# RWKV's weighted key-value scan on one core: constant rows by GpSimd's queue, later converting loads, and earlier state steps

## The chip, the cores and the metric

The kernel runs on one core of one Trainium2 chip. The metric is the device time of one execution in microseconds (us), lower is better. A core has a matrix engine (TensorE, PE in the profile), a vector engine (VectorE, DVE), a scalar engine for activations (ScalarE, ACT), GpSimd (POOL) and a fifth engine, SyncE (SP), which here only issues transfers. They run side by side and each works through its own list in order. Transfers between the chip's main memory and the on-chip memory are started by an engine that issues them and are then carried out by the core's 16 DMA engines.

## What is computed

For each of 16 sequences, 2048 steps and 256 channels, a weighted running mean of v is kept, with weights exp(k) that decay by w with each step; the current step has the extra weight u. The reference keeps the running maximum pp so that no exponential overflows:

```python
# w, u: [256]; k, v, output: [16, 2048, 256], all float32
for t in range(seq_len):
    ww = u + k[t]
    qq = max(pp, ww)
    output[t] = (exp(pp - qq) * aa + exp(ww - qq) * v[t]) / (exp(pp - qq) * bb + exp(ww - qq) + 1e-8)
    ww = pp - w + k[t]
    qq = max(ww, k[t])
    aa = exp(ww - qq) * aa + exp(k[t] - qq) * v[t]
    bb = exp(ww - qq) * bb + exp(k[t] - qq)
    pp = qq
```

## The kernel before

Time is cut into 16 chunks of 128 steps; a chunk of four sequences is one *slot*, so there are 64 slots, four to a chunk. In a slot n

- k and v (512 KB each) are loaded; k is rounded by DVE (`round_k`) and v converted to bf16 by DVE (`cast_v`), except that for every fourth slot from 11 on the transfer itself converts v[...];
- PE forms the exponents from k and from the rows of w and u (`logs`), ACT exponentiates them (`exps`), DVE multiplies by v (`times_v`);
- PE sums over half chunks (`sums`); once per chunk a chain of small operations on ACT, DVE, GpSimd and PE carries the state on (`copy_sums`, `turn`, `state_logs`, `state_frames`, `state_scan`, `state_offsets`, `state_weights`, `state_chain`, `turn_back`) and GpSimd injects it into rows of the exponentials by four small transfers (`inject`);
- ten slots later (LAG) PE forms denominator and numerator (`den`, `num`), ACT the reciprocal as Ln and Exp (`recip`), DVE the product (`mult`), and SP stores the result.

The parts that the change touches (cuts marked):

```python
AHEAD, LAG, RING = 6, 10, 12
kpool = ...tile_pool(name="kpool", bufs=AHEAD)
vpool = ...tile_pool(name="vpool", bufs=5)
vbpool = ...tile_pool(name="vbpool", bufs=4)        # v as bf16

def v_mode(n):
    return "dma" if n >= LAG and n % 4 == 3 else "dve"

def load_k(n, queue=SP): ...                         # 512 KB
def load_v(n, queue=SP):
    if v_mode(n) == "dma":
        VB[n] = vbpool.tile([128, 4, Dm], BF16, tag="vb", name="vb")
        K(POOL.dma_start(out=VB[n], in_=rows_of(v, n)))      # converts
    else:
        vr_of[n] = vpool.tile([128, 4, Dm], F32, tag="vr", name="vr")
        K(queue.dma_start(out=vr_of[n], in_=rows_of(v, n)))

def load(n):
    load_k(n)
    load_v(n)
# ...
K(POOL.memset(wuf, 0.0))
fill(idle, 0.0); fill(M1, -1.0); fill(I1, 0.0)       # fill: DVE memset
load_k(0, SP)
load_row(SC, 0, 0, w)                                # 2 rows of wuf
load_row(SP, 1, 2, u)
for n in range(1, AHEAD):
    load_k(n); load_v(n - 1)
# ... GpSimd: iota for COf, selects for M1, I1, COf (two)
# ... DVE: NLE and NLZ from M1 and I1, fills of Sel and OH, CO from COf
# ... GpSimd: six selects for Sel
# ...
def state_start(): ...       # DVE fills for the first chunk's state
def out_matrices(*names): ...# DVE: L, Id, LN, IdN from Lx and I1
# ...
idle_matmuls(10, MISC)
round_k(0)
fill(Lx, 1.0)                # and three selects on GpSimd
K(SC.activation(WU, wuf..., ACT.Copy))
logs(0); round_k(1); cast_v(0)
for n in range(LAG):
    load_v(n + AHEAD - 1)
    load_k(n + AHEAD)
    exps(n)
    if n % 4 == 0 and n: sums(n - 1)
    small_work(n, "act"); small_work(n, "logs")
    logs(n + 1)
    if n % 4: sums(n - 1)
    small_work(n, "pe")
    idle_matmuls(2, NUMB)
    times_v(n)
    small_work(n, "chain")
    round_k(n + 2)
    small_work(n, "round")
    cast_v(n + 1)
    if n == 2: state_start(); out_matrices("Id")
    if n == 6: out_matrices("L", "IdN", "LN")
load_v(LAG + AHEAD - 1)
for n in range(LAG, NP):
    if n + AHEAD < NP: load(n + AHEAD)
    # ... num, den, exps, recip, mult, round_k(n + 2), cast_v(n + 1),
    # ... store, times_v(n), logs(n + 1), sums; small_work between
# ... eleven more slots of outputs alone
```

`small_work(n, place)` runs the state steps that a plan puts in this place of slot n. For the first two chunks (slots 0 to 7) frames, scan and offsets are DVE's; later GpSimd has frames and offsets.

Of the kernel before, what the change touches and what calls it, by code (L numbers as in the profile page):

```python
# [15 lines left out]
def kernel(  # L16
# [10 lines left out]
    PE, DVE, SC, POOL, SP = nc.tensor, nc.vector, nc.scalar, nc.gpsimd, nc.sync  # L27

    B, T, Dm = k.shape
    HS = 64  # L30
# [3 lines left out]
    NP = 4 * NST  # L34
    RING = 12
    AHEAD = 6
    LAG = 10
# [16 lines left out]
    def v_mode(n):  # L54
        return "dma" if n >= LAG and n % 4 == 3 else "dve"

    def rows_of(x, n):
        c, p = divmod(n, 4)
        return x[4 * p:4 * p + 4, c * TC:(c + 1) * TC, :].rearrange("n t d -> t n d")

    def load_k(n, queue=SP):
        kr_of[n] = kpool.tile([128, 4, Dm], F32, tag="kr", name="kr")
        K(queue.dma_start(out=kr_of[n], in_=rows_of(k, n)))
# [4 lines that stand above are left out]
            K(POOL.dma_start(out=VB[n], in_=rows_of(v, n)))  # L68
        else:
            vr_of[n] = vpool.tile([128, 4, Dm], F32, tag="vr", name="vr")  # L70
            K(queue.dma_start(out=vr_of[n], in_=rows_of(v, n)))

    def load(n):
        load_k(n)
        load_v(n)

    def matrix(name, dt):
        return consts.tile([128, 128], dt, tag=name, name=name)  # L80

    def fill(ap, value):
        K(DVE.memset(ap.bitcast(F32) if ap.dtype == F32R else ap, value))

    GE, NE = ALU.is_ge, ALU.not_equal

    def select(ap, cmp, fill, base, cm, pattern):
        K(POOL.affine_select(out=ap, in_=ap, pattern=pattern, compare_op=cmp,
                             fill=fill, base=base, channel_multiplier=cm))

    M1, I1, Lx, COf = [matrix(x, F32) for x in ("M1", "I1", "Lx", "COf")]
# [3 lines left out]
    OH = consts.tile([128, 56], BF16, tag="OH", name="OH")  # L95
    Sel = consts.tile([128, 3, 2, 2, 4, 2], F32, tag="Sel", name="Sel")
    def load_row(eng, r, g0, x):
        K(eng.dma_start(out=wuf.rearrange("(g r) n d -> r g n d", r=32)[r, g0:4], in_=bass.AP(
            tensor=x.tensor, offset=x.offset, ap=[[0, 4 - g0], [0, 2], list(x.ap[0])])))
# [2 lines left out]
    fill(idle, 0.0)  # L102
    fill(M1, -1.0)
    fill(I1, 0.0)
    load_k(0, SP)
    load_row(SC, 0, 0, w)
    load_row(SP, 1, 2, u)
    for n in range(1, AHEAD):
        load_k(n)
        load_v(n - 1)  # L110
# [6 lines left out]
    for g in (2, 3):  # L117
        select(COf, NE, 1.0, -32 * g - 1, 1, [[0, 128]])


    NLE, NLZ, CO = matrix("NLE", F32R), matrix("NLZ", F32R), matrix("CO", F32R)
    K(DVE.tensor_scalar(NLE, M1, 0.5, None, ALU.add))
    for h in range(2):
        fill(NLE[HS * h:HS * h + HS, HS * (1 - h):HS * (2 - h)], 0.0)
    K(DVE.tensor_tensor(NLZ, NLE, I1, ALU.add))
    fill(Sel, 0.0)
    fill(OH, 0.0)
    for h in range(2):
        fill(OH[HS * h:HS * h + HS, 24 + h:25 + h], 1.0)
        fill(OH[HS * h:HS * h + 1, 32 + h:33 + h], 1.0)  # L130
    K(DVE.tensor_copy(CO, COf))
    for j, r in ((0, 0), (1, 8), (2, 64)):
        for h in range(2):
# [4 lines left out]
    def out_matrices(*names):  # L138
        if "L" in names:
            for h in range(2):  # L140
                fill(Lx[HS * h:HS * h + HS, HS * (1 - h):HS * (2 - h)], 0.0)
        for name in names:
            x, f = I1 if name[0] == "I" else Lx, RS if name[-1] == "N" else 1.0
            mats[name] = matrix(name, BF16)
            K(DVE.tensor_single_scalar(mats[name], x, f, op=ALU.mult))
# [18 lines left out]
    def round_k(n):  # L164
        km = consts.tile([128, 4, Dm], F32R, tag=f"km{n % 2}", name="km") if n < 2 else KM[n - 2]
        K(DVE.tensor_copy(km, kr_of.pop(n)))  # L166
        KM[n] = km
# [20 lines left out]
    def exps(n):  # L188
        if n < TURNS:
            for q in range(2):  # L190
                K(SC.activation(ez(n)[:, q], half(n, q), ACT.Exp))  # L191
        else:
            K(SC.activation(ez(n)[:, 0:2], PS[:, 0:4, :].rearrange("p (q i) x -> p q i x", q=2), ACT.Exp))  # L193
# [26 lines left out]
    def state_start():  # L220
        fill(CB_of[0], 0.0)
        K(DVE.memset(LL_of[0][:, 0, :, 0:1], -100.0))
        K(DVE.memset(LL_of[1][:, 1, :, 2:3], 0.0))
        for F in F_of:
            K(DVE.memset(F[:, :, 0:1], -1.0e30))
        K(DVE.memset(AB_of[0][:, :, 0, :], 0.0))
# [124 lines left out]
    def mult(n, bank, i):  # L351
        rd = RD[n]
        K(DVE.tensor_mul(rd[:, i, :], bank, rd[:, i, :]))  # L353
# [13 lines left out]
    for c in range(NST):  # L367
        s = 4 * c + 3
        plan = [(s + 1, "act" if s + 1 < LAG else "recip", copy_sums), (s + 1, "pe", turn),
                (s + 2, "act", state_logs), (s + 2, "mid", state_frames), (s + 2, "scan", state_scan), (s + 2, "scan", state_offsets),  # L370
                (s + 3, "recip", state_weights), (s + 3, "chain", state_chain),
                (s + 4, "nums", turn_back), (s + 4, "mid", inject), (s + 4, "mid", state_next)]
        if c == 0:
            plan = [(s + 1, "act", copy_sums), (s + 1, "pe", turn), (s + 2, "act", state_logs),
                    (s + 2, "round", state_frames), (s + 2, "round", state_scan), (s + 2, "round", state_offsets),
                    (s + 3, "act", state_weights), (s + 3, "round", state_chain),
                    (s + 4, "logs", turn_back), (s + 4, "logs", inject), (s + 4, "round", state_next)]
        if c == 1:
            plan = [(s + 1, "act", copy_sums), (s + 1, "pe", turn), (s + 2, "act", state_logs),
                    (s + 2, "round", state_frames), (s + 2, "round", state_scan), (s + 2, "round", state_offsets)] + plan[6:]  # L380
        if c == NST - 1:
            plan = [(s + 1, "copy", copy_sums), (s + 1, "turn", turn),
                    (s + 1, "post", state_logs), (s + 1, "mid", state_frames), (s + 1, "mid", state_scan), (s + 1, "mid", state_offsets),
                    (s + 2, "post", state_weights), (s + 2, "first", state_chain),
                    (s + 3, "turn", turn_back), (s + 3, "first", inject)]
        for slot, where, f in plan:
            later.setdefault((slot, where), []).append((f, c))

    def small_work(n, where):
        for f, c in later.pop((n, where), []):  # L390
            f(c)
# [4 lines left out]

    idle_matmuls(10, MISC)
    round_k(0)
    fill(Lx, 1.0)
    select(Lx, GE, 0.0, -1, -1, [[1, 128]])  # L400

    for h in range(2):
        select(Lx, NE, 1.0, -(HS * h + HS - 1), 1, [[0, 128]])
    K(SC.activation(WU, wuf.rearrange("p n d -> p (n d)"), ACT.Copy))
    logs(0)
    round_k(1)
    cast_v(0)
    for n in range(LAG):

        load_v(n + AHEAD - 1)  # L410
        load_k(n + AHEAD)
        exps(n)
        if n % 4 == 0 and n:
            sums(n - 1)
        small_work(n, "act")
        small_work(n, "logs")
        logs(n + 1)
        if n % 4:
            sums(n - 1)
# [4 lines that stand above are left out]
        round_k(n + 2)  # L424
        small_work(n, "round")
        cast_v(n + 1)
        if n == 2:
            state_start()
            out_matrices("Id")
        if n == 6:  # L430
            out_matrices("L", "IdN", "LN")
    load_v(LAG + AHEAD - 1)
    for n in range(LAG, NP):

        q, qp = n - LAG, n - LAG - 1
        if n + AHEAD < NP:
            load(n + AHEAD)
        if qp >= 0:
            num(qp, NUMB, 0)
        den(q)  # L440
        small_work(n, "nums")

        if n % 2 == 0:
            sums(n - 1)
        exps(n)
        small_work(n, "act")
        recip(q, lambda: small_work(n, "recip"))
        if qp >= 0:
            mult(qp, NUMB, 0)
        small_work(n, "mid")  # L450
        if n + 2 < NP:
            round_k(n + 2)
        if n + 1 < NP:
# [3 lines that stand above are left out]
        if qp >= 0:  # L457
            num(qp, NUMB, 1)
            mult(qp, NUMB, 1)
        small_work(n, "scan")  # L460
        if qp >= 0:
            store(qp)
        if n + 1 < NP:
# [4 lines that stand above are left out]
            den(q + 1)  # L468
        if n % 2:
            sums(n - 1)  # L470
        small_work(n, "pe")
# [58 lines left out]
```

## Time and profile before

| | |
|---|---|
| median time of 3 runs | 296.0 us (295.67 to 296.08) |
| span of the profiled execution | 293.2 us |
| read from and written to main memory | 67.12 MB, 33.55 MB |
| TensorE's granted clock, mean | 0.991 |
| SP: loads of k, loads of v, stores | 64, 50, 65 |
| GpSimd: converting loads of v, injections | 14, 64 |

In the profile's lines a row names line, engine, operation and tiles, `xN` counts instructions, and brackets tell how long the engine was idle before it and what ended the wait. `SPq` and `POOLq` are the sequencers of SP and GpSimd. In the stretches (from:to in us) the fields are the length, then busy time of PE, PEld (weight loads), DVE, ACT and POOL with counts, then TensorE's clock as a share of full speed, the DMA engines' busy share, and GB/s. For a converting load GB/s counts the 256 KB written, not the 512 KB read.

### The profile page before, as it was taken

To read this page: it belongs to the slowest core of one execution; us is meant where nothing else is said; L and a number is where in the kernel's file an instruction comes from. 1 tells how busy PE (TensorE), PEld (TensorE's weight loads), DVE (VectorE), ACT (ScalarE), POOL (GpSimd) and SP (SyncE) were. 2 spreads that over 40 slices of the span, in tenths; PEclk is the share of its full clock that TensorE was granted. 3 is DMA by queue.
4 is the path that set the end of the run, shared out by engine and by line. 5 is a ranking of instruction groups with operands and counts; after the bars stand their busy time and mean duration, and the time that the engine had idled before them with its cause. 6 is when DMAs were issued, how large, how long until landed. Compare 5 with 4: busy or idle time off the path is not lost. (4 is left out here: it accounts for less than half of the span.)

```text
span 293.2 us, 4973 instructions
## 1 busy us (share of the span) xinstructions
PE 268.6 (92%) x1694; PEld 122.5 (42%) x1694; DVE 257.4 (88%) x441; ACT 257.0 (88%) x253; POOL 117.4 (40%) x219
## 2 busy tenths in 40 slices
PE   7885599999999999999999999999999999998881
PEld 3342244445444444444444344544354344434330
DVE  3785989999999999999999999999999999886753
ACT  3765359999999999999999999999999999999892
POOL 5010061445555435344555545344455545242200
PEclk9999989999999999999999999999999999999998
DMA  6999999999999999999999999999999999954686
GB/s 190 355 348 312 357 333 324 334 342 379 330 383 329 385 331 385 351 361 379 334 377 333 383 331 386 334 380 356 355 380 337 379 338 385 380 206 151 215 290 215
DMA packets 103515, 97.86 MB, mean 334 GB/s; under 512 B 4150, under 2 KB 103490, under 8 KB 103490
## 3 DMA queue, kind: packets, MB, share of 16 engines
q1 hardware_dynamic: 93750, 93.08, 94.1%
q0 software_dynamic: 9440, 4.20, 9.9%
q8 instruction: 13, 0.21, 0.3%
q10 hardware_dynamic: 300, 0.27, 0.3%
q14 instruction: 12, 0.10, 0.1%
HBM read 67.12 MB, written 33.55 MB: 343 GB/s over the span
## 5 line engine op out<-in xcount | busy, mean ns | idle before, releaser
L193 ACT ACTIVATE EZR<-PS 128x2048 bf16<-128x2048 f32 x54 | 100.9, 1868 | 5.1 <-PE PS L180 3.1
L353 DVE TENSOR_TENSOR rd<-PS,rd 128x512 f32<-128x512 f32 (+1 forms) x118 | 86.4, 734 | 13.0 <-PE PS L349 10.1
L211 DVE TENSOR_TENSOR EZR<-EZR,vb 128x2048 bf16<-128x2048 bf16 x64 | 77.5, 1211 | 1.9 <-ACT EZR L191 1.2
L344 ACT ACTIVATE rd<-rd 128x1024 f32<-128x1024 f32 (+1 forms) x65 | 68.0, 1046 | 1.2
L326 POOL DMA_DIRECT2D EZR<-cb x64 | 39.0, 613 | 75.0 <-DVE cb L321 68.5
L342 ACT ACTIVATE rd<-PS 128x1024 f32<-128x1024 f32 (+1 forms) x65 | 65.5, 1008 | 1.6 <-PE PS L336 1.5
L166 DVE CAST km<-kr 128x1024 fp32r<-128x1024 f32 x64 | 44.4, 694 | 8.7 <-DMA kr<-in_k_dram 8.7
L180 PE MATMUL PS<-km,NLE 128*128 128x512 f32 x128 | 47.2, 450 | 5.0 <-DVE km L166 5.0
L349 PE MATMUL PS<-EZR,LN 128*128 128x512 bf16 x128 | 49.1, 383 | 2.8 <-DVE rd L353 0.8
L349 PE MATMUL PS<-EZR,IdN 128*128 128x512 bf16 x128 | 48.5, 379 | 0.0
L180 PE MATMUL PS<-km,NLZ 128*128 128x512 f32 x128 | 40.5, 398 | 0.0
L336 PE MATMUL PS<-EZR,L 128*128 128x512 bf16 x128 | 38.0, 379 | 1.8 <-ACT rd L342 1.8
L206 DVE CAST vb<-vr 128x1024 bf16<-128x1024 f32 x50 | 37.4, 747 | 2.0 <-DMA vr<-in_v_dram 2.0
L336 PE MATMUL PS<-EZR,Id 128*128 128x512 bf16 x128 | 38.1, 379 | 0.0
L175 PE MATMUL PS<-WU,CO 32*128 32x512 f32 x256 | 33.6, 495 | 0.9 <-ACT EZR L191 0.5
L266 POOL TENSOR_TENSOR F<-LL,LL 128x32 f32<-128x32 f32 x13 | 9.0, 695 | 50.3 <-ACT LL L257 50.3
L191 ACT ACTIVATE EZR<-PS 128x1024 bf16<-128x1024 f32 x20 | 19.4, 1020 | 10.9 <-PE PS L180 10.9
L180 PEld LDWEIGHTS PS<-km,NLE 128*128 128x128 f32 x128 | 19.0, 188 | 21.0 <-issue 14.0
L180 PEld LDWEIGHTS PS<-km,NLZ 128*128 128x128 f32 x128 | 24.3, 190 | 5.9
L235 PE MATMUL PS<-EZR,OH 128*32 128x256 bf16 x512 | 26.3, 282 | 0.5 <-DVE EZR L211 0.5
L175 PEld LDWEIGHTS PS<-WU,CO 32*128 32x128 f32 x256 | 12.8, 181 | 28.0 <-issue 13.3
L349 PEld LDWEIGHTS <-LN 128*128 128x128 bf16 x128 | 12.7, 99 | 19.0 <-issue 15.0
(67 smaller groups left out, 216.2 us busy)
## 6 DMA issues: line engine op xcount, KB each, us to landing
kr<-in_k_dram SPq DMA_DIRECT2D x64, 512.0 KB, 9.0
out_dram<-rd SPq DMA_DIRECT2D x63, 512.0 KB, 8.2
vr<-in_v_dram SPq DMA_DIRECT2D x50, 512.0 KB, 9.0
vb<-in_v_dram POOLq DMA_DIRECT2D x14, 256.0 KB, 8.3
EZR<-cb POOLq DMA_DIRECT2D x64, 8.0 KB, 5.2
out_dram<-rd SPq DMA_DIRECT2D x2, 128.0 KB, 2.9
out_dram<-rd ACTq DMA_DIRECT2D x2, 128.0 KB, 3.2
wuf<-in_u_dram SPq DMA_DIRECT2D x1, 4.0 KB
```

Of the source, the lines that this page charges most:

```text
L166: K(DVE.tensor_copy(km, kr_of.pop(n)))
L175: K(PE.matmul(half(n, q)[:, i, :], CO[g:g + 32, :], WU[g:g + 32, :], start=True, stop=False, tile_position=(g, 0), skip_group_check=True))
L180: K(PE.matmul(half(n, q)[:, i, :], (NLE, NLZ)[q], km[:, i, :], start=False, stop=True, skip_group_check=True))
L193: K(SC.activation(ez(n)[:, 0:2], PS[:, 0:4, :].rearrange("p (q i) x -> p q i x", q=2), ACT.Exp))
L206: K(DVE.tensor_copy(vb, vr))
L211: K(DVE.tensor_mul(ez(n)[:, 2:4], ez(n)[:, 0:2], vb.unsqueeze(1).broadcast_to([128, 2, 2, D])))
L326: K(POOL.dma_start(out=EZR[r:r + 1, 2 * q, r0:r0 + 4, :, :].rearrange("o p i (b x) -> o (p i b) x", b=4), in_=cb[x:x + 32, :]))
L336: K(PE.matmul(DENB[:, i, :], mats[m], ez(n)[:, q, i, :], start=q == 0, stop=q == 1, skip_group_check=True))
L342: K(SC.activation(rd[:, i, :], DENB[:, i, :], ACT.Ln, scale=RS))
L344: K(SC.activation(rd[:, i, :], rd[:, i, :], ACT.Exp, scale=-1.0))
L349: K(PE.matmul(bank, mats[m], ez(n)[:, q, i, :], start=q == 2, stop=q == 3, skip_group_check=True))
L353: K(DVE.tensor_mul(rd[:, i, :], bank, rd[:, i, :]))
```

## The change

It does five things. The row of w leaves ACT's queue and that of u leaves SP's; both are issued by GpSimd. The converting load for slot n is issued in slot n - 4 rather than in slot n - 6 (n - 5 for the first), so that it holds one of the four buffers for a shorter time. For the first two chunks, frames, scan and offsets (and the first chunk's chain) go ahead of `round_k` in DVE's list, in place of behind it. Constants for the output are made one piece a slot in slots 0 to 3, in place of in slots 2 and 6. Lx, Sel and OH are filled earlier.

```diff
     def load(n):
-        load_k(n)
-        load_v(n)
+        for x, f in ((n - 1, load_v), (n, load_k)) if n < LAG + AHEAD else ((n, load_k), (n, load_v)):
+            if x < NP and (f == load_k or v_mode(x) != "dma"):
+                f(x)
+        x = n - 2
+        if x < NP and v_mode(x) == "dma":
+            load_v(x)
@@
-    load_k(0, SP)
-    load_row(SC, 0, 0, w)
-    load_row(SP, 1, 2, u)
+    load_k(0)
+    load_row(POOL, 0, 0, w)
+    load_row(POOL, 1, 2, u)
@@ after the selects for M1, I1 and COf
+    fill(Lx, 1.0)
+    select(Lx, ...)                      # three selects, from further down
+    fill(Sel, 0.0)                       # and the fills of OH, from behind NLZ
@@ plan of chunk 0 (chunk 1 the same, without state_chain)
-                    (s + 2, "round", state_frames), (s + 2, "round", state_scan), (s + 2, "round", state_offsets),
-                    (s + 3, "act", state_weights), (s + 3, "round", state_chain),
+                    (s + 2, "chain", state_frames), (s + 2, "chain", state_scan), (s + 2, "chain", state_offsets),
+                    (s + 3, "act", state_weights), (s + 3, "chain", state_chain),
@@ in the loop over the first LAG slots
-        load_v(n + AHEAD - 1)
-        load_k(n + AHEAD)
+        load(n + AHEAD)
@@
-        if n == 2:
-            state_start()
-            out_matrices("Id")
-        if n == 6:
-            out_matrices("L", "IdN", "LN")
-    load_v(LAG + AHEAD - 1)
+        if n < 4:
+            (state_start, lambda: out_matrices("L"), lambda: out_matrices("IdN", "LN"),
+             lambda: out_matrices("Id"))[n]()
     for n in range(LAG, NP):
-        if n + AHEAD < NP:
-            load(n + AHEAD)
+        load(n + AHEAD)
```

More of the change, by code (lines that the diff above doesn't have):

```diff
@@ L118 @@
         select(COf, NE, 1.0, -32 * g - 1, 1, [[0, 128]])
+    fill(Lx, 1.0)
+    select(Lx, GE, 0.0, -1, -1, [[1, 128]])
+    for h in range(2):
+        select(Lx, NE, 1.0, -(HS * h + HS - 1), 1, [[0, 128]])
+    fill(Sel, 0.0)
+    fill(OH, 0.0)
+    for h in range(2):
+        fill(OH[HS * h:HS * h + HS, 24 + h:25 + h], 1.0)
+        fill(OH[HS * h:HS * h + 1, 32 + h:33 + h], 1.0)
     NLE, NLZ, CO = matrix("NLE", F32R), matrix("NLZ", F32R), matrix("CO", F32R)
@@ L125 @@
     K(DVE.tensor_tensor(NLZ, NLE, I1, ALU.add))
[L126 to L130, printed above, removed]
     K(DVE.tensor_copy(CO, COf))
@@ L379 @@
             plan = [(s + 1, "act", copy_sums), (s + 1, "pe", turn), (s + 2, "act", state_logs),
-                    (s + 2, "round", state_frames), (s + 2, "round", state_scan), (s + 2, "round", state_offsets)] + plan[6:]
+                    (s + 2, "chain", state_frames), (s + 2, "chain", state_scan), (s + 2, "chain", state_offsets)] + plan[6:]
         if c == NST - 1:
@@ L398 @@
     round_k(0)
[L399 to L403, printed above, removed]
     K(SC.activation(WU, wuf.rearrange("p n d -> p (n d)"), ACT.Copy))
```

## The prediction

> **What bounds the kernel now.** I read the page's busy shares first, then its 40 slices, then busy time in stretches of 10 us and of 1 us, then the timeline where a stretch looked thin, and last the loads one by one. The page alone names no single bound:
>
> ```profile
> PE 268.6 (92%) x1694; PEld 122.5 (42%) x1694; DVE 257.4 (88%) x441; ACT 257.0 (88%) x253; POOL 117.4 (40%) x219
> ...
> DMA  6999999999999999999999999999999999954686
> GB/s 190 355 348 312 357 333 324 334 342 379 330 383 329 385 331 385 351 361 379 334 377 333 383 331 386 334 380 356 355 380 337 379 338 385 380 206 151 215 290 215
> ```
>
> Three engines are near 90% and the transfers are at "9" from the second slice to the 34th (about 250 us), after which comes a tail of some 40 us with little to load. The stretches of 10 us (PE, PEld, DVE, ACT, POOL busy, granted clock, DMA share, GB/s) separate the stages:
>
> ```profile
> 20.00:30.00 10.00, 6.47 (x45) 3.61 (x45) 6.67 (x12) 4.68 (x7) 1.28 (x1) 1.00 1.14 324
> 30.00:40.00 10.00, 7.04 (x50) 2.83 (x49) 9.60 (x24) 4.51 (x6) 3.57 (x6) 0.83 1.10 353
> ...
> 100.00:110.00 10.00, 10.00 (x72) 4.53 (x74) 9.71 (x15) 9.69 (x10) 5.15 (x11) 1.00 1.14 346
> ...
> 240.00:250.00 10.00, 9.46 (x66) 3.98 (x64) 9.31 (x16) 9.29 (x9) 5.95 (x11) 1.00 1.10 380
> ```
>
> From 20 to 40 us PE is idle for 6.5 us and ACT for 10.8 us, PE's clock even falls to 0.83; yet the DMA share is the same 1.1 as everywhere. At 100 us PE, DVE and ACT are all full. At 240 us they have thinned again. The question is which of the two, transfers or engines, decides when the last rows of k can be used. The loads answer it:
>
> ```profile
> 49.10 1.18 SPq L63 DMA_DIRECT2D kr<-in_k_dram  x1
> ```
> ```profile
> 246.19 1.28 SPq L63 DMA_DIRECT2D kr<-in_k_dram  x1
> ```
> ```profile
> 254.34 0.69 DVE L166 CAST km<-kr 128x1024 fp32r<-128x1024 f32 x1 [0.38 <-DMA kr<-in_k_dram]
> ```
>
> Counting issues from the start, the first is k of slot 17, the second k of slot 63, the last. Slot 17 was rounded at 65.70 us, 16.6 us after its issue: a full four slots of lead. Slot 63 was rounded 8.15 us after its issue, and DVE waited for it. A load near the end takes this long to land (the view of the k tiles from 200 us on):
>
> ```profile
> DMA to landing us min/median/max: 7.9/8.9/10.1
> ```
>
> So the lead has been eaten. Between those two issues the queue advanced (246.19 - 49.10) / 46 = 4.28 us a slot, while the engines, where undisturbed, need 4.07 (the four injections at 66.08, 82.38 and 98.67 us stand 16.3 us apart, per four slots). The transfers are slower than the engines, so the engines catch up and from about 200 us on run at the transfers' pace. My reading: **the instant 254.3 us is set by the transfers**, which have been saturated since about 3 us, and the 293.2 - 254.3 = 38.9 us after it by the engines' tail (the chain of waits shows PE and ACT handing over to each other there).
>
> **What the skill says.** The Trainium skill, "DMA: Bandwidth & Descriptors", section "Issuing engines are not separate DMA queues", says that transfers started by any engine end up on the same 16 DMA engines and interleave, so that another queue saves only the sequencer's issue time. The trace agrees: during a converting load from GpSimd's queue (data at 106 to 110 us) counted traffic falls from about 380 to 262-302 GB/s. "Perfetto Trace Analysis", section "Identifying the Most-Contended Engine", says that DMA occupancy misleads and that HBM utilization should be used; so I rest on GB/s and on lead per load, not on the digit 9. "TensorE: Matmul & The Clock Gate", section "What's actually happening", says the clock depends on how busy PE has recently been, with half speed after an idle window of about 3.4 us: the 0.83 here follows two idle stretches of PE close together, 2.11 us (to 29.27) and 2.96 us (to 34.30), each shorter than the window the page names.
>
> **The change, part by part.**
>
> (a) *u leaves SP's queue.* Today k of slot 0 is issued at 0.79, u at 1.34 for 0.69 us, and only then k of slot 1 at 2.07. In stretches of 1 us the transfers show the hole:
>
> ```profile
> 3.00:4.00 1.00, 1.00 (x4) 0.39 (x3) 0.83 (x8) 1.00 (x1) 0.61 (x4) 1.00 1.08 380
> 4.00:5.00 1.00, 1.00 (x4) 0.30 (x2) 0.16 (x2) 0.06 (x1) 0.75 (x4) 1.00 1.04 182
> 5.00:6.00 1.00, 0.57 (x6) 0.19 (x4) 0.71 (x2) 0.63 (x1) 0.22 (x1) 1.00 0.89 284
> ```
>
> Later stretches that hold loads alone give 347 GB/s. Over 3 to 8 us they moved 380+182+284+358+341 = 1545 KB where 5 x 347 = 1735 would fit: 190 KB, or 0.55 us. With k of slot 1 issued 0.7 us earlier the hole closes: **-0.6 us** for every transfer behind it, and that lasts to 254 us.
>
> (b) *w and u on GpSimd.* Two issues there, each some 0.6 us (0.50 to 0.62 us is the mean for the four small injections), stand ahead of the iota and the selects, and Sel's six selects (1.25 us) now come between the two for COf. CO, ready at about 4.0 us now, would be at about 6; the rows, landed at 5.0 now, at 4 to 7 (the small injections from GpSimd land 1.7 us after issue at the shortest, 5.2 at the median). The first exponentials start at 6.9 us and could slip to 8 or 9. They are not on the path yet: DVE's first product waits for v of slot 0 (cast at 8.74) until 9.5. A slip of 0 to 1.5 us, caught up at 3.0 us of transfer time a slot against about 2.6 us of DVE work (1.22 + 0.69 + 0.69). Loads do not stop, because six buffers of k and five of v lie ahead: **0**.
>
> (c) *Converting loads at slot n for n+4.* The first, for slot 11, now goes out after the product of slot 2 (20.5 us) and its 256 KB pass at 25 to 29 us, just where rounding waits for k:
>
> ```profile
> 23.91 0.69 DVE L166 CAST km<-kr 128x1024 fp32r<-128x1024 f32 x1 [1.07 <-DMA kr<-in_k_dram]
> ```
> ```profile
> 28.52 0.69 DVE L166 CAST km<-kr 128x1024 fp32r<-128x1024 f32 x1 [1.99 <-DMA kr<-in_k_dram]
> ```
>
> Issued in slot 7 it moves behind these loads, so some 1.5 to 3 us of waiting goes. In the steady part GpSimd issues it after the state offsets (about 111.5 us in the stage shown) instead of after the state update (102.1); it lands by 120, needed at 132. No bytes are saved: **0 at the end**, -2 us in the engines' early part.
>
> (d) *Frames, scan, offsets and chain ahead of the rounding.* The 1.5 us of eight small DVE operations (29.13 to 30.6) move into the 1.99 us in which DVE waited, and the state's matrix is ready before PE asks:
>
> ```profile
> 34.30 0.40 PE L315 MATMUL PS<-Id,CB 128*128 128x128 bf16 x4 [2.96 <-DVE CB L299]
> ```
>
> This 2.96 us of PE, the clock drop behind it, and ACT's 3.23 us before 36.03 go or shrink.
>
> (e) *Constants in slots 0 to 3.* About 0.7 us of DVE leaves slot 6 for slots with slack. Work is moved, none removed.
>
> (c) to (e) together let the engines reach slot 10 perhaps 4 to 6 us sooner than 43.7 us. But then they only meet the transfers sooner: lead falls to the landing time near slot 25 rather than near slot 45. What of it reaches the end is that loads are no longer held up for buffers around 41 to 44 us, where 328+308+301 = 937 KB moved instead of 3 x 347 = 1041: **-0.3 us**. Sum: -0.6 - 0.3 = -0.9 us, with the tail of 38.9 us unchanged: 296.0 - 0.9 = 295.1, say **295.0 us**.
>
> **Rivals.** *The engines are the bound* (R1): then the 4 to 6 us pass through to the end, for 290 to 292 us. For it speak PE's 10.00 of 10 at 100 us and waits for loads of only 3.3 us in all after 45 us; against it, the lead that shrank from 16.6 to 8.15 us and the thinner stretches after 200 us. *GpSimd becomes the wait* (R2): rows of w and u land late, or the injections queue behind a converting load and come after slot 4c+10 needs them. Today the last of four lands at about 105.9 us, needed at 109.0; by my working the new load is already in by 119.8 when the next four land at about 122, needed at 125.3. Were they 1 us late in each of 13 rounds, it would be 13 us: 305 to 309. *The late converting load delays the last k* (R3): that of slot 63 now moves at about 247-251 instead of 237-241 us, beside k of slot 63. The bytes before that k are the same, so I expect nothing; at worst one load's 1.4 us: 296 to 297.
>
> **Range and chances.** Between the transfer bound and R1 lie 3 to 5 us, and I hold the bound for much likelier; a part of R1 can come through if the transfers have slack that I don't see. Range 292.5 to 296.6. Over 2% faster means below 290.1, which needs all of R1: 0.07. Over 2% slower, above 301.9, needs R2: 0.03. Within 2%: 0.90.
>
> **What would show it.** Right: no hole at 4 to 6 us; slot 10 reached by 37 to 40 us with PE's clock at 1.0 throughout; more waits of rounding for k in the middle (3.3 us grows to 6 or more); the last k rounded at about 253.4 us; a tail of about 39 us. (a) is wrong if the last k comes no earlier; the bound is wrong if it is rounded before 252 us, or if the middle still shows a full lead. R2 would show as PE waiting for the injected rows at the product with L.

## The result and the profile after

| | before | changed |
|---|---|---|
| median, first comparison | 296.02 us (4 runs) | 294.36 us (4 runs) |
| ratio, first comparison | | 0.9948, 95% interval 0.9931 to 0.9966 |
| median, repeated later (see the fifth experiment) | 295.28 us | 294.32 us |
| ratio, repeated | | 0.9971, 95% interval 0.9960 to 0.9983 |
| span of the profiled execution | 293.2 us | 292.9 us |

The changed kernel is 0.3 to 0.5% faster, by 1.0 to 1.7 us; 295.0 us had been predicted, 1.0 us under the 296.0 of the kernel before. The first trace of the kernel before belongs to an execution of 294.87 us, more than 1 us under its median, so the two spans differ less than the medians.

The page of the changed kernel, its granted clock and its transfers:

```profile
PE 270.0 (92%) x1694; PEld 123.9 (42%) x1694; DVE 254.3 (87%) x441; ACT 256.7 (88%) x253; POOL 120.7 (41%) x221
...
PEclk9699999999999999999999999999999999999997
DMA  7999999999999999999999999999999999954686
GB/s 219 348 348 349 321 335 324 340 361 346 383 319 382 331 383 334 384 345 370 374 339 382 331 384 337 377 369 344 375 332 385 333 384 347 369 203 151 220 286 215
```

The first slice rose from 190 to 219 GB/s, and the slices after it keep the old level: the gain is at the start. TensorE's clock is low in the second slice, which it was not before. In stretches of 10 us (columns as before):

```profile
0.00:10.00 10.00, 5.23 (x15) 1.69 (x15) 4.07 (x18) 1.91 (x2) 6.51 (x22) 0.96 0.85 254
10.00:20.00 10.00, 10.00 (x48) 5.10 (x48) 6.61 (x16) 6.27 (x7) 0.00 (x0) 0.70 1.10 348
20.00:30.00 10.00, 8.90 (x72) 4.22 (x71) 9.79 (x23) 8.18 (x11) 1.21 (x1) 1.00 1.10 348
30.00:40.00 10.00, 8.69 (x63) 4.46 (x64) 9.62 (x17) 6.33 (x8) 4.73 (x7) 1.00 1.14 327
...
200.00:210.00 10.00, 8.79 (x57) 4.26 (x56) 7.77 (x11) 8.16 (x9) 4.20 (x8) 1.00 1.08 376
```

From 20 to 40 us PE is idle for 2.4 us where it was 6.5, and ACT works 14.5 us where it worked 9.2. But from 0 to 10 us ACT works only 1.9 us in place of 4.7. The waits of the changed kernel say why, and show where the engines' advance is given back:

```profile
ACT WU L411 <- DMA wuf<-in_u_dram: 6.5, 1, 6.5
...
DVE km L178 <- DMA kr<-in_k_dram: 4.5, 6, 1.6
DVE EZR L223 <- ACT EZR L203: 4.4, 1, 4.4
```

(The columns are microseconds in total, times, longest.) The row of u is what ACT waits for at the start (6.5 us), and DVE in turn waits 4.4 us for the first exponentials. Rounding waits for k for 4.5 us, all of it late: the longest, 1.6 us, is the dip at 200 to 210 us. The hole of the first microseconds is closed (last column, GB/s):

```profile
3.00:4.00 1.00, 1.00 (x4) 0.39 (x3) 0.00 (x0) 0.00 (x0) 0.82 (x4) 1.00 0.98 348
4.00:5.00 1.00, 1.00 (x3) 0.30 (x2) 0.77 (x4) 0.00 (x0) 1.00 (x5) 1.00 1.09 384
5.00:6.00 1.00, 0.70 (x2) 0.00 (x0) 0.04 (x1) 0.00 (x0) 1.00 (x6) 1.00 1.10 357
```

SP issues almost without a pause from the start to the last load, so its issuing could be taken for the bound in place of the transfers. Two issues of 512 KB loads speak against it:

```profile
2.38 0.51 SPq L63 DMA_DIRECT2D kr<-in_k_dram  x1
108.69 1.28 SPq L63 DMA_DIRECT2D kr<-in_k_dram  x1
```

Early on an issue takes 0.51 us, later 1.28 us for the same load. And a load of k lands 9.2 us after its issue (median), while 512 KB at 347 to 385 GB/s take an estimated 1.4 to 1.5 us: about six transfers are in line at any time. SP is ahead of them and held up by them.

The last load of k and its rounding, from the timelines of SP and DVE:

```profile
244.22 1.24 SPq L63 DMA_DIRECT2D kr<-in_k_dram  x1
```
```profile
253.99 0.69 DVE L178 CAST km<-kr 128x1024 fp32r<-128x1024 f32 x1 [0.59 <-DMA kr<-in_k_dram]
```

It is issued 2.0 us sooner than before and rounded 0.35 us sooner, again after a wait. From there to the end are 292.9 - 254.0 = 38.9 us, as before.

### The profile page after: what moved, and what is told of

Same layout as the page of the kernel before. It is cut to its first block, busy times and chain, and to the rows that moved or that the text cites. A ratio compares the mean times of both kernels' runs of the same rounds, so it can differ in the third digit from the quotient of the medians.

```text
span 292.9 us, 4960 instructions
## 1 busy us (share of the span) xinstructions
PE 270.0 (92%) x1694; PEld 123.9 (42%) x1694; DVE 254.3 (87%) x441; ACT 256.7 (88%) x253; POOL 120.7 (41%) x221
## 5 line engine op out<-in xcount | busy, mean ns | idle before, releaser
L338 POOL DMA_DIRECT2D EZR<-cb x64 | 38.3, 604 | 54.4 <-DVE cb L333 40.2
L192 PE MATMUL PS<-km,NLE 128*128 128x512 f32 x128 | 48.0, 457 | 1.2 <-DVE km L178 1.2
L218 DVE CAST vb<-vr 128x1024 bf16<-128x1024 f32 x50 | 34.8, 697 | 0.5 <-DMA vr<-in_v_dram 0.5
L247 PE MATMUL PS<-EZR,OH 128*32 128x256 bf16 x512 | 25.6, 278 | 0.0
```

What stands on the lines that cost most here:

```text
L192: K(PE.matmul(half(n, q)[:, i, :], (NLE, NLZ)[q], km[:, i, :], start=False, stop=True, skip_group_check=True))
L218: K(DVE.tensor_copy(vb, vr))
L338: K(POOL.dma_start(out=EZR[r:r + 1, 2 * q, r0:r0 + 4, :, :].rearrange("o p i (b x) -> o (p i b) x", b=4), in_=cb[x:x + 32, :]))
```

## The experiments

"Changed" below is the changed kernel. Ratios are to the kernel before, run beside each on the same chip, with 95% intervals. "k of slot 17" and "the last k" are rounding times in the trace.

**Rows alone (e1).** The kernel before with the rows moved:

```diff
-    load_row(SC, 0, 0, w)
-    load_row(SP, 1, 2, u)
+    load_row(POOL, 0, 0, w)
+    load_row(POOL, 1, 2, u)
```

> The kernel before with the rows of w and u alone moved to GpSimd's queue. Transfers as the bound: every transfer behind k of slot 0 comes 0.6 us earlier and the late rows (in the changed kernel the weights were ready at 8.5 us in place of 5.0) are not felt at the end: 295.4 us, the last k rounded 0.6 us sooner than in the kernel before. Engines as the bound: the first exponentials slip by some 4 us and this, less what DVE's slack gives back, stays to the end: 297 to 299 us.

294.55 us against 295.16, ratio 0.9980 (0.9968 to 0.9992): 0.6 us faster. k of slot 17 is rounded at 67.64 us, 4.4 us later than in the changed kernel's first trace; the last k comes at 254.47 us, only 0.5 us later:

```profile
245.51 1.28 SPq L63 DMA_DIRECT2D kr<-in_k_dram  x1
254.47 0.68 DVE L166 CAST km<-kr 128x1024 fp32r<-128x1024 f32 x1
```

Its load was issued 0.68 us sooner than in the kernel before (246.19), with the same order of loads, and landed 8.2 us later, at 253.7 us, where the kernel before had it at 254.3. But the rounding has no wait in its brackets, nor has any after 60 us in this trace: here the engines arrive last, 0.8 us after the load has landed, and the last k is rounded no earlier than in the kernel before. The traced execution took 295.44 us, 0.9 us above the median of this version. It shows how close the two limits lie, not where the typical execution gains its 0.6 us.

**All but the rows (e2).** Changed, with `load_row(SC, 0, 0, w)` and `load_row(SP, 1, 2, u)` back.

> The changed kernel with w back on ACT's queue and u back on SP's. Transfers as the bound: the hole at 4 to 6 us comes back, so 0.6 us slower than the changed kernel: 295.0 us, although the first exponentials start 4 us sooner. Engines as the bound: the 4 us of the sooner start pass through: 291 to 292 us.

295.16 against 295.16 us, ratio 1.0002 (0.9987 to 1.0017). The rows are ready at 4.8 us again, and still nothing is gained: parts (c) to (e) alone are worth nothing at the end, to within the interval of some 0.5 us. Rounding still waits for k in slots 6 to 10, 2.3 us in all; in the kernel before it was 3.1. The last k waits 0.66 us and is rounded at 254.23 us.

**Both rows by ACT's queue (e3).**

```diff
-    load_row(POOL, 0, 0, w)
-    load_row(POOL, 1, 2, u)
+    load_row(SC, 0, 0, w)
+    load_row(SC, 1, 2, u)
```

> The changed kernel with both rows on ACT's queue: no hole on SP, and no late rows. Transfers as the bound: as the changed kernel, 294.1 to 294.6 us, with the engines 3 to 4 us ahead at slot 0 and level with it by the last k. Engines as the bound: 290.5 to 292 us.

294.18 us, ratio 0.9968 (0.9959 to 0.9978): as the changed kernel, to 0.2 us. One expectation was wrong. ACT's timeline shows u as late as from GpSimd:

```profile
2.60 0.56 ACTq L104 DMA_DIRECT2D wuf<-in_u_dram  x1
3.19 1.28 ACT L117 ACT_TABLE_LOAD   x1 [3.19 <-POOL COf L94]
8.44 0.63 ACT L411 ACTIVATE WU<-wuf 128x512 fp32r<-128x512 f32 x1 [3.97 <-DMA wuf<-in_u_dram]
```

Issued at 2.60, it releases ACT at 8.44. The lateness is not GpSimd's: on either queue, a few KB issued once SP has queued its first large loads took about 6 us. That they wait among these loads fits, but was not tested apart.

**The kernel before, again (e4).** Unchanged.

> The kernel before, unchanged, for a second trace: the one on record belongs to an execution of 294.9 us, 1.1 us under the median. Expected 296.0 us; transfers as the bound: its last k is rounded about 1 us later than the 254.3 us of that trace, with the tail after it the same 38.9 us. Engines as the bound: the extra 1 us lies anywhere, the lead of the last k over 10 us.

295.17 us. Last k issued at 246.25 and rounded at 254.46 us after a wait of 0.41: as in the first trace to 0.1 us. Why its median was 0.8 us higher in the first comparison than in the later ones is not settled.

**The changed kernel, again (e5).** Unchanged.

> The changed kernel, unchanged, beside the others. Expected 294.2 to 294.5 us if the kernel before takes 295.2 to 296.0 beside it. Transfers as the bound: the last k is rounded at 253.5 to 254.0 us after a wait. Engines as the bound: no wait there.

294.32 against 295.28 us. Last k at 253.42 us after a wait:

```profile
253.42 0.69 DVE L178 CAST km<-kr 128x1024 fp32r<-128x1024 f32 x1 [0.57 <-DMA kr<-in_k_dram]
```

k of slot 17 is rounded at 64.13 us, 0.9 us later than in the first trace (PE's clock was at half until 19 us here, not 16); this is the scatter to allow for.

**Stores two slots later (e6).** The test of the transfers as the bound, with nothing left out:

```diff
-rpool = ...tile_pool(name="rpool", bufs=6)
+rpool = ...tile_pool(name="rpool", bufs=8)
-        y = tiny.tile([128, 2, 32], F32, tag="y", name="y")
+        y = tiny.tile([128, 2, 32], F32, tag="x", name="y")
-            store(qp)
+            pending.append(qp)                   # pending = [] ahead of the loop
+            while len(pending) > (2 if n + AHEAD < NP else 0):
+                store(pending.pop(0))
```

> The changed kernel with each store two slots later in SP's list as long as loads are issued (8 result buffers in place of 6, and y shares x's buffer to make room); the same work and the same bytes, but two stores fewer ahead of the last k. Transfers as the bound: a store takes about 1.06 us of transfer time (4.08 us a slot with, 3.02 without, at 385 and 347 GB/s), so the last k is rounded 2.1 us sooner and the time falls to 292.2 to 292.8 us. Engines as the bound: nothing, 294.0 to 294.6 us.

292.49 us, ratio 0.9915 (0.9902 to 0.9928), 1.8 us under the changed kernel beside it. The last k:

```profile
251.33 0.69 DVE L178 CAST km<-kr 128x1024 fp32r<-128x1024 f32 x1 [0.45 <-DMA kr<-in_k_dram]
```

253.42 - 251.33 = 2.1 us for two stores, the 1.06 us apiece that the traffic gave. The two added result buffers are not what helps: no engine waits for such a buffer in the two traces of the changed kernel. After 60 us rounding waits for k once, for those 0.45 us, where the changed kernel beside it waited 3.1 us: with the transfers ahead, the engines are nearly the bound.

**Lighter engines (e7).** It leaves out, in slots 17 to 53, the second half of the numerators with its products, and the Exp of the reciprocals; all transfers stay:

```diff
-            K(SC.activation(rd[:, i, :], rd[:, i, :], ACT.Exp, scale=-1.0))
+            if not 6 <= n < 43:
+                K(SC.activation(rd[:, i, :], rd[:, i, :], ACT.Exp, scale=-1.0))
-        if qp >= 0:
+        if qp >= 0 and not 6 <= qp < 43:
             num(qp, NUMB, 1)
             mult(qp, NUMB, 1)
```

> The changed kernel with work left out in 37 of its slots (17 to 53): half of the numerators and of their products, and the Exp of the reciprocals, that is some 0.77 us of PE, 0.73 us of DVE and 1.05 us of ACT a slot; all transfers stay, so the stored values of these slots are not the results. Transfers as the bound: DVE's waits for k grow from 4.5 us to over 20, the last k is rounded at 253 to 254 us and the time stays at 294 to 294.5 us. Engines as the bound: 37 slots at 0.7 to 1.0 us each, 257 to 268 us.

294.43 us, ratio 0.9975 (0.9964 to 0.9986): the changed kernel's time, with 35 us less of ACT's busy time (221.8 in place of 256.8). Its waits from 60 us on, and two of its stretches:

```profile
DVE km L178 <- DMA kr<-in_k_dram: 23.1, 16, 2.5
ACT rd L354 <- DMA out_dram<-rd: 4.7, 6, 1.4
```
```profile
200.00:210.00 10.00, 7.36 (x47) 3.14 (x47) 7.18 (x14) 6.35 (x7) 4.86 (x8) 1.00 1.09 383
240.00:250.00 10.00, 9.50 (x67) 3.98 (x66) 9.85 (x19) 9.06 (x10) 7.11 (x12) 1.00 1.13 354
```

At 200 us PE, DVE and ACT are 64 to 74% busy, and the transfers run at 383 GB/s, where the changed kernel had 376. What the engines no longer do has become waiting for k, 23.1 us, and the last k is rounded at 253.72 us.

**Rows by ACT and stores later (e8).** e3 and e6 together.

> Both rows on ACT's queue (as in the run with rows by ACT) and the stores two slots later. Transfers as the bound: the two gains add, 292.0 to 292.6 us. Engines as the bound: as the run with rows by ACT, within 0.2 us.

292.14 us, ratio 0.9896 (0.9884 to 0.9909). This is the best version here, 1.0% under the kernel before and computing the same.

**Converting loads as before (e9).** Changed, with the old distances:

```diff
-        for x, f in ((n - 1, load_v), (n, load_k)) if n < LAG + AHEAD else ((n, load_k), (n, load_v)):
-            if x < NP and (f == load_k or v_mode(x) != "dma"):
-                f(x)
-        x = n - 2
-        if x < NP and v_mode(x) == "dma":
-            load_v(x)
+        if n <= LAG + AHEAD:
+            load_v(n - 1)
+        if n < NP:
+            load_k(n)
+        if LAG + AHEAD <= n < NP:
+            load_v(n)
```

> The changed kernel with the converting loads issued as in the kernel before (six slots ahead, five for the first). Transfers as the bound: the first converting load again passes in front of the loads of k for slots 6 and 7, so DVE waits 1 to 3 us more before slot 8 and k of slot 17 is rounded 0.5 to 2 us later than in the changed kernel (64.1 us in its second trace); at the end nothing of it is left, the last k at 253.2 to 253.9 us, 294.1 to 294.6 us. Engines as the bound: the 0.5 to 2 us pass through, 295 to 296 us. The late converting load as a cost at the end (third rival): the last k comes 0.5 to 1.4 us sooner without it, 293 to 293.8 us.

294.33 us, ratio 0.9976 (0.9968 to 0.9984): no difference at the end. Nor is there one early: k of slot 17 at 62.97 us, and no wait for k before slot 8. What changes is the form of the late waits:

```profile
DVE km L176 <- DMA kr<-in_k_dram: 7.4, 18, 1.3
```

Eighteen waits of mostly 0.2 to 0.5 us, where the changed kernel has six, one in four slots, each at the k that travels beside a converting load. The last k is issued at 245.59 us, 0.60 us before that of the kernel before with the same order of loads (246.19), and rounded at 253.72 us.

**State steps and constants as before (e10).** Changed, with `"chain"` back to `"round"` for the first two chunks and the constants back in slots 2 and 6.

> The changed kernel with the state steps of the first two chunks behind the rounding of k again, and the constants in slots 2 and 6 again; rows and converting loads stay changed. Transfers as the bound: k of slot 17 is rounded 1.5 to 3 us later than in the changed kernel (66 to 67 us), later waits for k shrink by as much, and the time is 294.3 to 294.7 us. Engines as the bound: 295.8 to 297.3 us.

294.49 us, ratio 0.9978 (0.9965 to 0.9991). k of slot 17 at 66.16 us, 2.0 to 2.9 us later than in the two traces of the changed kernel; one wait for k after 60 us, 0.4 us, in place of five or six; the last k at 253.52 us.

## Why the prediction was right, and where it was not

**The bound was right.** The transfers set the time of the last k in the changed kernel, and the engines only the 39 us after it. e7 takes more than 30 us off ACT and the time stays; e6 takes two stores from before the last k and the time falls by what two stores cost. The first rival is out for the changed kernel: advances of 2 to 4 us by slot 17 are gone by slot 63 (e10, e1). It keeps a part: in e1's trace the engines took (254.47 - 67.64) / 46 = 4.06 us a slot without a wait, the pace that the prediction had named, and came 0.8 us after the last k had landed. The engines' limit is just behind that of the transfers, and a further gain on one side soon meets the other, as e6 does.

**(a) was right in mechanism, and in size for the traces it was read from.** From 3 to 8 us 348+384+357+342+344 = 1775 KB moved in place of 1545, and 230 / 347 is 0.66 us. The last k was issued 0.60 us sooner (e9) and 0.68 us sooner (e1) where the order of loads is the same, and the rows alone gave 0.6 us of the median (e1), against nothing for all the rest without them (e2). A last k that comes no earlier was to speak against (a); in e1's trace it is rounded no earlier, but its load landed 0.6 us sooner and the engines were late. The hole is not the same in every execution: the three traces with u on SP's queue moved 1545 KB, 1391 (e4) and 1419 (e2) from 3 to 8 us, the nine with the rows moved 1760 to 1797. Against the changed kernel that makes 0.7 to 1.1 us.

**(b) was right at the end and far off in size.** A slip of 0 to 1.5 us was written; the first exponentials came 4.3 us later (kernel before, then changed):

```profile
6.91 1.94 ACT L191 ACTIVATE EZR<-PS 128x1024 bf16<-128x1024 f32 x2 [1.26 <-PE PS L180]
11.21 1.94 ACT L203 ACTIVATE EZR<-PS 128x1024 bf16<-128x1024 f32 x2 [2.04 <-PE PS L192]
```

The step that failed is the landing of the rows. Taken from the small injections (1.7 to 5.2 us after issue), it had been put at 4 to 7 us; u landed 6.1 us after its issue, and ACT could start on the rows only at 8.54 us. PE then stood idle for 3.5 us and its clock was at half until 16 us, where 1.0 throughout had been predicted. It cost nothing at the end, for the reason given: loads went on into free buffers. But this had been said of at most 1.5 us; that it held for 4.3 us as well was luck. The engines then ran the slots up to the sixth in 2.4 to 3.1 us each; by slot 7, where the kernel before had its stall, they were level (exponentials at 30.87 us; 30.89 before).

**(c) failed as to the early waits.** They would shrink by 1.5 to 3 us, it said. With the rows moved they are gone anyway (e9, and e1 without any of (c) to (e)): the engines' late start leaves the loads far enough ahead. With the rows where they were, (c) to (e) together shortened them by 0.8 us (e2). At the end it was 0, as predicted. The third rival is out: with the converting load of slot 63 late or early the last k is rounded at 253.4 to 254.0 or at 253.7 us.

**(d) and (e)** brought 2 to 3 us by slot 17 (e10), of the 4 to 6 us predicted for (c) to (e) together; PE's wait for the state's matrix fell from 2.96 to 0.94 us. The exponentials of slot 10 came at 41.08 us (43.70 before), not at 37 to 40. With the smaller advance the lead also shrank later than said: it is still 13.7 us at slot 24 and 10.4 at slot 40, in place of gone near 25, and rounding first waits for k at slot 43 and, in the second trace, 50 (in the two traces of the kernel before, once the early waits are over, at 51 and 52; its lead at slot 45, said to be gone there, was still 11.2 us). Those waits came to 4.5 and 3.1 us, not 6.

**The term of -0.3 us has no support.** It was to come from fuller transfers at 41 to 44 us; the changed kernel has a like dip at 39 to 42 us (333, 325, 296 GB/s). The differences of the changed kernel to e1, e9 and e10 are within their intervals. So of the sum of -0.9 us the 0.6 is shown, and that the sum comes near the later comparison's 1.0 us is in part luck. The rest of the measured 1.0 to 1.7 us is not assigned: the median of the kernel before alone moved by 0.8 us between comparisons, and though the hole was wider in its second trace, the last k was issued no later there (246.25 us against 246.19).

**The second rival** came true by half: the rows were late, the injections were not (PE has no wait for a transfer in the changed kernel's trace).

## What to carry to other kernels

When all engines and the transfers look full, follow single loads from issue to use: a lead that shrinks to the landing time tells that the transfers set the pace, though the engines wait for them almost nowhere. In this kernel only what put fewer bytes, or fewer idle microseconds of the transfers, ahead of the last load counted, and reordering the engines' work did not. In a list that mixes loads and stores, holding two stores back while loads are issued was worth nearly their transfer time (1.8 of 2.1 us); beyond that the engines are about to take over.

## What was not expected of the hardware

A transfer of 4 or 8 KB issued at 1.6 to 2.4 us by GpSimd's queue landed after 5.4 and 6.1 us, and one from ACT's queue at 2.60 us released ACT after 5.8 us, while w, issued by ACT at 1.35 us in the kernel before, had released ACT by 5.03 us. So the delay goes with what was queued before, rather than with the queue that issues. The Trainium skill ("DMA: Bandwidth & Descriptors", section "Issuing engines are not separate DMA queues") says that transfers of all engines interleave on the same DMA engines, which fits a like delay on both queues.
